# Bidirectional RWKV-7 scan on one core: operands kept at their rows, products as 64x64 quarters and column halves, and a written order for TensorE

## The chip, the cores and the metric

The kernel runs on 1 core of one Trainium2 chip. The metric is device time in microseconds (us), the median of several runs. Before the change it is 1737.47 us, the median of 3 runs that lie between 1731.84 and 1740.01.

## The reference

One layer of a hybrid denoising network works on 128 context tokens and 2048 latent tokens of width 1024. Both sets are RMS-normalised, modulated by a conditioning vector and sent through one input projection. Half of the channels (8 heads of 64) go through RWKV-7 time mixing in both directions in time, the other half through a gated short convolution. The output projection, the residual and a last RMS norm follow. What the change is about is the recurrence over time:

```
def step(S, inp):
    r_t, w_t, k_t, v_t, kk_t, a_t = inp
    s_kk = jnp.einsum('bdhij,bdhj->bdhi', S, kk_t)
    S = (S * w_t[..., None, :] - s_kk[..., :, None] * (kk_t * a_t)[..., None, :]
         + v_t[..., :, None] * k_t[..., None, :])
    return S, jnp.einsum('bdhij,bdhj->bdhi', S, r_t)
...
s_final, ys = lax.scan(step, s0.astype(f32), xs)
...
y = ys[:, 0] + jnp.flip(ys[:, 1], axis=1)
```

A state S is 64x64 for each head and direction. The sum of both directions is normalised by head, weighted, gated and handed to the output projection. The results are y for both token sets and the final context states.

## The kernel before

**Three phases.** Phase 1 does the norms, the input projection, the gates and the low-rank products, and writes what the scan needs to DRAM: `ops{d}` (four operands of each direction d, channel by token, scaled by running products of the decay), `pc{d}` (the decay over a chunk), `vt` (the values, token by channel), `sg`, `q` and the convolution's half of `mixT`. Phase 2 is the scan. Phase 3 multiplies `mixT` by the output weights (psu, lines L1300 to L1302), adds the residual and norms. Each weight there is split into a high and a low part, so a product is three matmuls.

**Stages of the scan.** The scan takes chunks of 64 tokens. A stage is 8 chunks of one pair of heads in both directions (`gi` 0 and 1 are the directions), and there are 17: 16 for the latent tokens, and one, at place 15, for the context of all heads. A stage has six pieces of work:

- partL (L866 on) loads the stage's operands into `rr`, 128 partitions for the two heads of 64 channels.
- partM: ACT copies two operands into block-diagonal 128x128 tiles `bd` (make_bd, a copy for each head), so that one matmul can do both heads. TensorE makes F (psF) and G (psG) of each chunk, both at L905, which DVE masks into `F` and `GA`; it transposes one operand into `Q` (psQ, L898). GA's last 64 columns hold A, the in-chunk interaction of the delta rule. ACT and DVE pick A's diagonal 32x32 blocks (`dg`, L910), and a DMA writes them to DRAM.
- partI: POOL reads all 32x32 blocks of the stage (`ab`) and inverts them as triangular matrices (`zt`, L927 to L948, most of it at L944 and L947). A DMA on POOL's queue writes the inverses to DRAM. partM and partI run LA = 3 stages ahead of the scan.
- partW and partU: the stacked operands `stl` and `str` get their rows from DRAM and, by ACT copies, from GA and Q. `zc` fetches the inverses. psU (L1005) and psW (L1012), 32x32 products in two row tiles, join two 32-blocks into the inverse of a 64-block, which ACT copies into the block-diagonal `zb`.
- partB: psX (L1031) is the inverse times F, copied negated into stl or str by ACT (L790, and L792 for plain copies). psE (L1042) is stl times str, 128x128 for a chunk and head, and DVE masks it into `E` (L1043).
- partS: the scan. psS (L1067) is E times `sv`, whose rows hold the chunk's values and the incoming state. Its one half is the state out, which DVE scales by `pc` into the next chunk's sv (L1080); the other is the chunk's output, added into `y`. When a block of tokens has both directions, finish() does the group norm and transposes y (psT, L1145).

Each psum bank holds four chunks or two chunks of two heads; the pools p2 (psU, psW, psX, psE, psT) have 2 banks, pS (psS) 4, pm (psF, psG, psQ) 2.

**What sets the order.** main() (from L1172) takes a stage's 8 scan steps and between them lets the generators of the other pieces go on: of this stage the rest of partB, of the next stage partW, partU and the first of partB, of stage s+3 partM, and a pending finish. ORDER, ORDER_END and MORD say how many pieces after which step. The order in which each engine then runs its instructions is set by the scheduler of the Tile framework, which simulates a timeline. In the last three stages phase 3 begins: weights() loads the four convolution weights (CONV), ahead() does the convolution half of the products of the first AHEAD = 3 output tiles (psa), and tail() does the rest of the 17 tiles.

Of the kernel before, what the change touches and what calls it, by code (L numbers as in the profile page):

```python
# [6 lines left out]
F32 = mybir.dt.float32  # L7
# [41 lines left out]
def phase1(K):  # L49
# [285 lines left out]

    npair = [0]
# [13 lines left out]
    def mixA(g, j, ws, hh, lw, pre):  # L350

        t0, n = BLK[j]
        nch = n // 64
        tl = lambda tag, b=1: (tp if tag == "sg" else ta_).tile([128, 384], F32, tag=tag, name=f"{tag}_{g}_{j}_{K.u()}", bufs=b)
# [16 lines left out]
        for d in range(2):  # L371
# [32 lines left out]
            nc.scalar.dma_start(S[f"pc{d}"][g * 128:(g + 1) * 128, t0 // 64:t0 // 64 + nch], pt[:, :nch, 64 - 64 * d])  # L404
# [10 lines left out]
            kds.append(kd)  # L415
        bs = kds[0]
# [7 lines left out]
    def gateA(g, j, ws, hh, bsum):  # L424

        t0, n = BLK[j]
        tl = lambda tag, b=1: (tp if tag == "sg" else ta_).tile([128, 384], F32, tag=tag, name=f"{tag}_{g}_{j}_{K.u()}", bufs=b)
# [16 lines left out]
        nc.sync.dma_start(S["vt"][t0:t0 + n, g * 128:(g + 1) * 128].rearrange("(a p) c -> p a c", p=128), vt[:, :n // 128])  # L444
# [242 lines left out]
for _d in range(2):  # L687
    SCR[f"ops{_d}"] = (4, 512, NT)
    SCR[f"pc{_d}"] = (512, 34)
SCR.update(vt=(NT, 512), sg=(512, NT), q=(512, NT), mixT=(1024, NT))  # L690
# [4 lines left out]
MORD = ("Ff", "GgD", "", "Q")  # L695
ON_DVE = ""
# [3 lines left out]
ORDER_END = ('LbbbL', 'UU', 'U', '', 'BBB', '', '', '', '')  # L700
ORDER = ('LbbbL', '', 'U', 'U', 'U', '', 'BBB', '', '')


def phase2(K):
# [3 lines left out]
    MF, MG, ME = (0, 1), (0, 1), (2, 3)  # L708
    B = Ctx()
    O = Ctx()  # L710
    O.scaled = None

    def setup_first():

        O.r0 = Pool(K, "p2r0", "right")
        O.rI = Pool(K, "p2rI", "right")
        O.r1 = Pool(K, "p2r1", "right")
        O.pm = Pool(K, "p2m", "right", 2, PSUM)
        B.msk = O.r0.tile([128, 4, 128], F32, name="msk")
        B.mkg = O.r0.tile([128, 2, 128], F32, name="mkg")  # L720
        for i, j in enumerate((0, 2, 4, 5)):
            D(B.msk[:, i], A["msk"][:, j, 0:128])
        for i, j in enumerate((1, 3)):
            D(B.mkg[:, i], A["msk"][:, j, 64:192])
# [6 lines left out]
        B.slots = []  # L731
        for i in range(2):
            new_slot(O.r0)
        B.bd = ring(O.r1, 2, [128, 8, 128], "bd", zero)
        B.rr = ring(O.r1, 2, [128, 5, 8, 64], "rr", presetR)

    def new_slot(pool):
        i = len(B.slots)
        B.slots.append([tuple(pool.tile([128, 8, w], F32, tag=f"{n}{i}{d}", name=f"{n}{i}{d}", bufs=1) for n, w in (("F", 128), ("GA", 128), ("Q", 64))) for d in range(2)])

    def spare(i, name, dt):

        tags = ["F10", "GA10", "F11", "GA11", "F00", "F01", "GA00", "GA01"]
        if i >= 8:
            return O.rI.tile([128, 1024], dt, tag="ab", name=name, bufs=2)
        return O.r0.tile([128, 1024], dt, tag=tags[i], name=name, bufs=1)

    def setup_rest():
        O.l0 = Pool(K, "p2l0", "left")
        O.l1 = Pool(K, "p2l1", "left")  # L750
        O.p2 = Pool(K, "p2s", "left", 2, PSUM)
        O.pS = Pool(K, "p2S", "left", 4, PSUM)
        O.r2 = Pool(K, "p2r2", "right")
        new_slot(O.r2)
# [8 lines left out]
        for d in range(2):  # L763
            D(B.pc[:, d], S[f"pc{d}"].rearrange("(e c) n -> c e n", c=64))

        lt = ring(O.l1, 2, [128, 2, 8, 128], "stl", lambda t_: presetS(vl(t_)))
        rt = ring(O.l1, 2, [128, 2, 2, 8, 64], "str", presetS)
        B.lt, B.rt = lambda: vl(lt()), rt
        B.bu = O.l1.tile([128, 16, 32], F32, name="bu")
        B.zb = O.l1.tile([128, 2, 8, 128], F32, name="zb")  # L770
        zero(B.zb)

    def ring(pool, n, shape, name, init=None):
        l = [pool.tile(shape, F32, name=f"{name}{i}") for i in range(n)]
        if init:
            for t_ in l:
                init(t_)
        st = [0]

        def get():  # L780
            st[0] += 1
            return l[(st[0] - 1) % n]
        return get

    def copy(k, dst, src, negate=False):
        if negate:
            if k in ON_DVE:
                V.tensor_scalar(dst, src, -1.0, None, ALU.mult)
            else:
                P.activation(dst, src, AF.Copy, scale=-1.0)  # L790
        else:
            (V.tensor_copy if k in ON_DVE else P.copy)(dst, src)  # L792

    def zero(t_):
        G.memset(t_[:], 0.0)

    i2b = lambda n: B.I2[:].unsqueeze(1).broadcast_to((128, n, 64))

    def presetR(t_):
        V.tensor_copy(t_[:, 2], i2b(8))  # L800

    def vl(t_):
        return t_[:].rearrange("p h u (b t) -> p b h u t", b=2)

    def presetS(t_):
        for hd in range(2):
            V.tensor_copy(t_[0:64, 0, hd], B.I2[0:64].unsqueeze(1).broadcast_to((64, 8, 64)))
# [11 lines left out]
    def load(dst, d, k, units, part):  # L819

        a, b = part.start, part.stop
        p, c0 = units[0]
        n = len(units)
        src = S[f"ops{d}"][k]
        if p == units[-1][0]:
            D(dst[part], src[p * 128 + a:p * 128 + b, c0 * 64:(c0 + n) * 64].rearrange("p (u t) -> p u t", t=64))
        else:
            src = src[p * 128:(p + n // 2) * 128, 0:128].rearrange("(g p) t -> p g t", p=128)[part]
            for u in range(2):
                D(dst[part].rearrange("p (g u) t -> p u g t", u=2)[:, u], src[:, :, u * 64:u * 64 + 64])  # L830

    def load_v(dst, units):
        if units[0][0] == units[-1][0]:
            p, c0 = units[0]
            D(dst.rearrange("t u h v -> t u (h v)"), S["vt"][c0 * 64:(c0 + 8) * 64, p * 128:(p + 1) * 128].rearrange("(u t) c -> t u c", t=64))
        else:
            for u in range(2):
                D(dst.rearrange("t (g u) h v -> t u g (h v)", u=2)[:, u], S["vt"][u * 64:u * 64 + 64, :].rearrange("t (g c) -> t g c", g=4))

    H0, H1, FULL = slice(0, 64), slice(64, 128), slice(0, 128)  # L840

    def make_bd(t_, src):
        copy("b", t_[0:64, :, 64:128], src[0:64])
        copy("c", t_[64:128, :, 0:64], src[64:128])

    def load_stk(t_, g, k, us):

        units = g.units[us]
        p, c0 = units[0]
        src = S[f"ops{g.d}"][k]  # L850
        n = 4 if p == units[-1][0] else 2
        for i in range(4 // n):
            dst = t_[0:64, 1, :, us.start + n * i:us.start + n * (i + 1)]
            x = src[(p + i) * 128:(p + i + 1) * 128, c0 * 64:(c0 + n) * 64]
            if t_ is g.rt:
# [571 lines left out]
```

## Time and profile before

| | |
|---|---|
| median of 3 runs | 1737.47 us |
| profiled execution, its own time | 1726.64 us |
| its span | 1724.9 us |
| mean granted TensorE clock | 0.970 |
| TensorE matmul (PE) busy | 1640.9 us, 95% |
| VectorE (DVE), ScalarE (ACT), GpSimd (POOL) busy | 64%, 50%, 34% |
| first scan matmul to last | 1017.3 to 1561 us |

The profile is of one execution. PEld is TensorE's weight load, which runs beside PE. Groups are named by line, engine, operation and `out<-in`, with the busy time and the mean duration of one instruction, and then the engine's idle time ahead of them with what ended it. Matmuls are pipelined, so a duration is longer than the distance from one start to the next. The granted clock is the share of full speed that TensorE was allowed. Rows of the timeline have a start, a length and, in brackets, the idle time before them and its releaser.

### The profile page before, as it was taken

Reading aid. Unit: us, or ns where it says so; the run is one execution under the profiler, and the core shown is the slowest. Engines: PE = TensorE matmul, PEld = TensorE weight load, DVE = VectorE, ACT = ScalarE, POOL = GpSimd, SP = SyncE. Lnnn points to the kernel's source line nnn. Section 1 sums busy time; section 2 is a strip of 40 time slices with the busy share of each in tenths; the row PEclk is TensorE's granted clock in tenths of the full one; section 3 lists DMA queues with packets and bytes.
Section 4 is the critical chain, followed back from the end, with each engine's and each line's share of the span. In section 5 each row is a group of like instructions: output and inputs, shape, how many; then the busy total and the mean of one; then the engine's idle time right before and its main releaser. Section 6 shows DMA issues by size and latency. Waiting matters only on the chain. (4 is left out here: it accounts for less than half of the span.)

```text
span 1724.9 us, 32848 instructions
## 1 busy us (share of the span) xinstructions
PE 1640.9 (95%) x12400; PEld 1556.2 (90%) x12400; DVE 1107.3 (64%) x2092; ACT 868.8 (50%) x1719; POOL 587.4 (34%) x1089
## 2 busy tenths in 40 slices
PE   5989899999999999999999989999999999999998
PEld 2889889899999999999999989999999999887886
DVE  5875778775568858587854344666766656646433
ACT  4533454443243534244423187788878777643222
POOL 0010111111110201021213737877877768223221
PEclk8899999999999999999999999899999989899999
DMA  9687778675557657567896376677878874746442
GB/s 372 212 221 235 223 245 252 199 234 183 173 182 209 176 173 188 167 188 248 208 304 218 112 191 154 163 185 186 203 186 189 189 177 106 195 153 202 147 147 92
DMA packets 314286, 335.66 MB, mean 195 GB/s; under 512 B 165448, under 2 KB 262344, under 8 KB 300048
## 3 DMA queue, kind: packets, MB, share of 16 engines
q1 hardware_dynamic: 277184, 328.97, 65.3%
q10 hardware_dynamic: 35584, 0.14, 1.3%
q0 software_dynamic: 1360, 4.46, 0.7%
q8 instruction: 98, 1.61, 0.4%
q14 instruction: 60, 0.49, 0.1%
HBM read 221.42 MB, written 112.08 MB: 193 GB/s over the span
## 5 line engine op out<-in xcount | busy, mean ns | idle before, releaser
L947 POOL TENSOR_TENSOR zt<-zt,ztmp 128x30 f32<-128x30 f32 (+7 forms) x510 | 198.6, 389 | 39.3
L1067 PE MATMUL psS<-sv,E 128*128 128x64 f32 x1088 | 154.4, 277 | 0.0
L1067 PEld LDWEIGHTS psS<-sv,E 128*128 128x128 f32 x1088 | 145.4, 200 | 1.9
L1042 PE MATMUL psE<-str,stl 128*128 128x128 f32 x1088 | 140.8, 278 | 5.4 <-DVE E L1043 3.8
L944 POOL TENSOR_TENSOR ztmp<-ab,zt 128x60 f32<-128x60 f32 (+7 forms) x255 | 133.5, 524 | 19.4
L1042 PEld LDWEIGHTS psE<-str,stl 128*128 128x128 f32 x1088 | 129.8, 192 | 7.1 <-DVE E L1043 4.8
L323 POOL TENSOR_TENSOR shk<-rawl 128x384 f32<-128x384 f32 (+1 forms) x24 | 23.0, 959 | 322.6 <-ACT rawl L319 322.6
L1080 DVE TENSOR_TENSOR sv<-psS,pc 64x128 f32<-64x128 f32 x254 | 69.4, 277 | 97.3 <-PE psS L1067 96.9
L792 ACT COPY bd<-rr 64x512 f32<-64x512 f32 x136 | 84.0, 617 | 77.2 <-issue 24.5
L1043 DVE TENSOR_TENSOR E<-psE,msk 128x512 f32<-128x512 f32 x136 | 92.9, 685 | 27.6 <-PE psE L1042 26.9
L905 PE MATMUL psF<-rr,bd 128*128 128x128 f32 x544 | 78.8, 291 | 13.0 <-ACT Q L792 10.6
L1363 POOL TENSOR_TENSOR z<-z,x 128x512 f32<-128x512 f32 x32 | 43.6, 1364 | 126.5 <-DVE z L1359 105.8
L905 PEld LDWEIGHTS psF<-rr,bd 128*128 128x128 f32 x544 | 69.2, 199 | 16.3 <-ACT Q L792 13.1
L1031 PE MATMUL psX<-F,zb 128*128 128x128 f32 x544 | 80.7, 303 | 2.7 <-ACT zb L790 1.7
L323 POOL TENSOR_TENSOR shv<-rawl 128x384 f32<-128x384 f32 (+1 forms) x24 | 22.3, 930 | 178.2 <-ACT rawl L319 172.9
L905 PE MATMUL psG<-rr,bd 128*128 128x128 f32 x544 | 74.8, 286 | 2.9 <-DVE F L906 2.9
L1031 PEld LDWEIGHTS psX<-F,zb 128*128 128x128 f32 x544 | 73.7, 214 | 3.6 <-ACT zb L790 2.4
L160 PE MATMUL mmc<-h,w 128*128 128x384 f32 (+1 forms) x192 | 66.7, 347 | 6.8 <-ACT ta L397 3.4
L905 PEld LDWEIGHTS psG<-rr,bd 128*128 128x128 f32 x544 | 68.2, 199 | 3.3 <-DVE F L906 3.0
L161 PE MATMUL mmc<-h,w 128*128 128x384 f32 (+1 forms) x192 | 65.5, 341 | 0.0
L162 PE MATMUL mmc<-h,w 128*128 128x384 f32 (+1 forms) x192 | 65.4, 340 | 0.0
L160 PE MATMUL mmgb<-h,w 128*128 128x384 f32 (+1 forms) x192 | 64.4, 335 | 0.4 <-ACT q1r L321 0.4
(307 smaller groups left out, 5177.2 us busy)
## 6 DMA issues: line engine op xcount, KB each, us to landing
w<-scr_wsp SPq DMA_DIRECT2D x68, 1024.0 KB, 6.7
scr_wsp<-w SPq DMA_DIRECT2D x34, 1024.0 KB, 9.0
rr<-scr_ops SPq DMA_DIRECT2D x64, 512.0 KB, 4.4
scr_ops<-pair SPq DMA_DIRECT2D x80, 384.0 KB, 6.7
wr<-in_win SPq DMA_DIRECT2D x34, 512.0 KB, 6.1
ab<-scr_at SPq DMA_DIRECT2D x34, 256.0 KB, 3.8
x<-in_x SPq DMA_DIRECT2D x17, 512.0 KB, 3.7
wadas<-in_wada SPq DMA_DIRECT2D x8, 1024.0 KB, 14.1
```

Source lines behind the costliest of these rows:

```text
L160: T.matmul(ps[:, :n], w[:, 0, k], hh[:, 0, k, :n], start=k == 0, stop=False)
L161: T.matmul(ps[:, :n], w[:, 0, k], hh[:, 1, k, :n], start=False, stop=False)
L162: T.matmul(ps[:, :n], w[:, 1, k], hh[:, 0, k, :n], start=False, stop=k == 7)
L792: (V.tensor_copy if k in ON_DVE else P.copy)(dst, src)
L905: T.matmul(ps[:, i, :].rearrange("p (a b) -> p a b", b=64), w[:, u, :], x[:, :, u, :], start=True, stop=True)
L944: G.tensor_tensor(tv, ab[:, j:j + 2, j + 2:32].unsqueeze(1).broadcast_to((128, kn, 2, n)), zt[:, :kn, j:j + 2].unsqueeze(3).broadcast_to(( ...
L947: G.tensor_tensor(zt[:, :kn, j + 2:32], zt[:, :kn, j + 2:32], tv[:, :, r], ALU.subtract)
L1031: T.matmul(px[:, i, :], B.zb[:, gi, us.start + i, :], g.F[:, us.start + i, :], start=True, stop=True)
L1042: T.matmul(pe[:, i, hd, :].rearrange("p (b t) -> p b t", b=2), g.lt[:, :, hd, us.start + k + i].rearrange("p b t -> p (b t)"), g.rt[:, :, ...
L1043: V.tensor_tensor(g.E[n][:, k:k + 2].rearrange("p a b c -> p (a b) c"), pe[:].rearrange("p a b c -> p (a b) c"), B.msk[:, ME[g.d]].unsquee ...
L1067: T.matmul(sp[gi][:, q, hd, :], g.E[n][:, k, hd, :], sv[:, u, hd, :], start=True, stop=True)
L1080: r = V.tensor_tensor(dst, sp[gi][0:64, q], B.pc[0:64, d, 2 * p:2 * p + 2, c:c + 1].broadcast_to((64, 2, 64)), ALU.mult)
```

## The change

**Operands at their rows.** rr, bd, stl, str, F and GA slots and Q go. `B.ops` is a ring of four pairs of tiles that hold two operands of a stage, and `B.fg` holds for each direction, for the two sides of E, an identity block and two alternating slots of operands that load_half reads from DRAM a half stage at a time.

**64x64 quarters.** F, G, X and A are made for one head at a time, each head's matmul with 64 rows of weights and 64 columns of the array; place() gives the heads of one direction the straight quarters and those of the other the crossed ones. In the order of issue, both directions and both heads stand side by side, four quarters in turn. The G product's first block is the identity, and so brings what the Q transposes brought. A is a product of its own (psA), made in partM, the only piece left there; F and G move from three stages ahead into the stage before.

**Halves.** E and S are made as two 64-column halves of the array, each with half of the weight columns. ACT copies E's left half, which needs no mask, and DVE masks the right half.

**The order of TensorE.** mm() and tr() tie each matmul of the scan to the one issued before it, by a dependency without a semaphore, so that the scheduler keeps them in the written order. ROUND gives that order for a stage: S is one scan step of both directions, L in turn F and G of the first and second half of the next stage, b and B partB of this and of the next stage (X, or one group of E), u the transpose of the inverses and psU psW in turn with U, A partM, f three pieces of finish and T the rest of it.

**Buffers and queues.** p2 gets 3 banks and pS 3; zt 3 buffers (2 before), the A blocks' dg 2 (1). The chunk decays pc go by a POOL copy into a tile and one SP DMA for each pair of token blocks; before, 48 DMAs on ACT's queue. vt is stored by head pair, two DMAs of 64 partitions for one.

**Phase 3.** The convolution weights are loaded and split one at a time in ahead(), AHEAD falls to 2 tiles, and what frees them buffers changes.

```diff
-MORD = ("Ff", "GgD", "", "Q")
-ORDER_END = ('LbbbL', 'UU', 'U', '', 'BBB', '', '', '', '')
-ORDER = ('LbbbL', '', 'U', 'U', 'U', '', 'BBB', '', '')
+ROUND = "f A b L L S u b S b S L S U S L U S T S B S B B".split()
+ROUND_END = "f b L L u S b S b S L U S L S U S T S B B B S".split()
...
-    O.p2 = Pool(K, "p2s", "left", 2, PSUM)
-    O.pS = Pool(K, "p2S", "left", 4, PSUM)
+    O.p2 = Pool(K, "p2s", "left", 3, PSUM)
+    O.pS = Pool(K, "p2S", "left", 3, PSUM)
...
+    def behind(r, ins):
+        if ins is not None:
+            tc.add_manual_dep(r.ins, ins.name, mybir.DependencyInfo(mybir.DependencyClass.NoSync, mybir.DependencyReason.DATA), reason="order")
+    def mm(*a, **k):
+        r = T.matmul(*a, start=True, stop=True, **k)
+        if O.line:
+            behind(r, O.last)
+            O.last = r.ins
...
+    def place(d, h):
+        return H[1 - h if d == 0 else h]
...
     def partM(s, st):
+        pa = [O.pm.tile([128, 8, 64], F32, tag="m", name=f"psA{s}_{gi}") for gi in range(2)]
+        for u in range(8):
+            for gi, g in enumerate(st.g):
+                for h in range(2):
+                    mm(pa[gi][place(g.d, h), u, :], g.ops[H[h], 1, u, :], g.ops[H[h], 0, u, :])
+        yield
...
+            P.activation(dg[:], pa[gi][:, :, 0:32], AF.Identity, scale=B.hm[:, 0:1])
+            V.scalar_tensor_tensor(dg[:], pa[gi][:, :, 32:64], B.hm[:, 1:2], dg[:], ALU.mult, ALU.add)
+            copy(st.low[:, gi], pa[gi][:, :, 32:64])
+            D(at[gi * 8:gi * 8 + 8].rearrange("u s b j i -> (s b j) u i"), dg[:])
...
     def partW(s, st):
+            def product(k, x, nm):
+                ps = [O.p2.tile([128, 4, 128], F32, tag="s", name=f"ps{nm}{s}_{gi}_{n}") for gi in range(2)]
+                for i in range(4):
+                    for gi, g in enumerate(st.g):
+                        u = half(g, n).start + i
+                        for h in range(2):
+                            mm(ps[gi][place(g.d, h), i, :].rearrange("p (b t) -> p b t", b=2), g.ops[H[h], k, u, :], B.fg[g.d][H[h], x, g.io, h, u])
+                return ps
+            ps = product(0, 1, "F")
...
+            ps = product(1, 0, "G")
+            for gi, g in enumerate(st.g):
+                us = half(g, n)
+                for h in range(2):
+                    r = place(g.d, h)
+                    copy(g.gs[H[1 - h], 0, h, us], ps[gi][r, :, 0:64])
+                    V.tensor_tensor(g.gs[H[1 - h], g.op, h, us], ps[gi][r, :, 64:128], B.msk[r, MG[g.d], 64:128].unsqueeze(1).broadcast_to((64, 4, 64)), ALU.mult)
...
     def partB(s, st):
...
+                        for hd in range(2):
+                            for x in range(2):
+                                mm(pe[H[x], i, hd, :].rearrange("p (b t) -> p b t", b=2), lt[:, x * g.op, hd, u], rt[:, g.io, hd, u])
...
+                    copy(to(H[0]), of(H[0]))
+                    V.tensor_tensor(to(H[1]), of(H[1]), B.msk[:, ME[g.d], 64:128].unsqueeze(1).broadcast_to((128, 4, 64)), ALU.mult)
...
     def partS(s, st, nxt):
...
-                    T.matmul(sp[gi][:, q, hd, :], g.E[n][:, k, hd, :], sv[:, u, hd, :], start=True, stop=True)
+                    for x in H:
+                        mm(sp[gi][x, q, hd, :], g.E[n][:, k, hd, x], sv[:, u, hd, :])
...
-    AHEAD = TILES[:3]
+    AHEAD = TILES[:2]
```

On PE, in the scan of stage 7, the order before is the scheduler's. The names are psum tile, stage, direction (0 or 1) and half; the tiles after the arrow are the operands, and the last figures their shape and a count.

```order
L1067 MATMUL psS7_0_0_12996<-sv_1027_12520,E_1041_12802 128x64 x2
L1031 MATMUL psX7_1_1_12951<-F11_8820,zb_9831 128x128 x4
L1067 MATMUL psS7_1_0_13000<-sv_1028_12529,E_1042_12810 128x64 x2
L905 MATMUL psF10_1_0_13067<-rr1_8828,bd0_8823 128x128 x4
L905 MATMUL psF10_1_1_13073<-rr1_8828,bd0_8823 128x128 x3
L1067 MATMUL psS7_0_0_12996<-sv_1027_12520,E_1041_12802 128x64 x2
L905 MATMUL psF10_1_1_13073<-rr1_8828,bd0_8823 128x128
L1042 MATMUL psE7_0_10_12958<-str0_9824,stl0_9818 128x128 x4
```

After the change, at the same place of the same stage, PE's order reads:

```order
L780 MATMUL psG8_0_0_13947<-fg0_9774,o00_8854 64x128 x2
L780 MATMUL psG8_1_0_13948<-fg1_9775,o01_8855 64x128 x2
L780 MATMUL psS7_0_0_13973<-sv_1063_13382,E_1073_13710 64x64 x4
L780 MATMUL psS7_1_0_13979<-sv_1064_13384,E_1074_13713 64x64 x4
L780 MATMUL psE7_0_10_13987<-fg0_9774 64x128 x8
L780 MATMUL psE7_1_10_13998<-fg1_9775 64x128 x8
L780 MATMUL psS7_0_0_13973<-sv_1063_13382,E_1073_13710 64x64 x4
L780 MATMUL psS7_1_0_13979<-sv_1064_13384,E_1074_13713 64x64 x4
```

F and G of stage 10 stood between the scan steps of stage 7; now it is those of stage 8, pairs of quarters of the two directions follow each other, and groups of E stand whole between whole scan steps.

ACT has, before, this stretch of copies around the same scan steps (L790 negates, L792 copies; w and yss belong to finish):

```order
L790 ACTIVATE stl0_9818<-psX7_0_0_12803 64x2x4x64 x2
L790 ACTIVATE str1_9825<-psX7_1_0_12811 64x2x256 x2
L1128 ACTIVATE w_1054_13038<-y_1018_12326 128x512
L1132 ACTIVATE yss_1056_13054<-yss_1056_13054,geps_9813 128x8
L792 COPY bd1_8824<-rr1_8828 64x8x64 x2
L792 COPY str0_9824<-Q20_9805 64x2x2x64
L792 COPY str0_9824<-GA20_9804 64x256 x2
L792 COPY str0_9824<-Q20_9805 64x2x2x64
```

After, ACT's order at the start of stage 7's round is this (a0 takes A's lower blocks, which psU needs; fg takes both X and G):

```order
L771 COPY E_1074_13713<-psE7_1_01_13761 128x4x64
L839 ACTIVATE dg_1083_13878<-psA10_0_13844,hm_8852 128x256
L839 ACTIVATE dg_1084_13883<-psA10_1_13845,hm_8852 128x256
L771 COPY a0_8862<-psA10_0_13844 128x256
L771 COPY a0_8862<-psA10_1_13845 128x256
L769 ACTIVATE fg0_9774<-psX7_0_1_13888 64x2x256 x2
L769 ACTIVATE fg1_9775<-psX7_1_1_13889 64x2x256 x2
L972 ACTIVATE zb_9784<-zc_1089_13922,hm_8852 128x16x32 x2
L771 COPY fg0_9774<-psG8_0_0_13947 64x256
```

The copies into bd and from Q are gone, the two reads of A, four of X and the halves of E are the group that stands there now; all but zb read a psum bank.

More of the change, by code (lines that the diff above doesn't have):

```diff
@@ L805, in presetS @@
-    def presetS(t_):
-        for hd in range(2):
-            V.tensor_copy(t_[0:64, 0, hd], B.I2[0:64].unsqueeze(1).broadcast_to((64, 8, 64)))
+            P.activation(dst, src, AF.Copy, scale=-1.0)
+        else:
+            P.copy(dst, src)
+    def behind(r, ins):
[6 more added lines that the diff above has]
+            O.last = r.ins
@@ L809, in tl, with tr @@
+    def tr(*a):
+        r = T.transpose(*a)
+        if O.line:
+            behind(r, O.last)
+            O.last = r.ins
     def tl(shape, tag, b, pool=None, dt=F32):
@@ L817, in phase2 @@
     stages.insert(15, [(d, [(u // 2, u % 2) for u in range(8)], None) for d in range(2)])
[L819 to L855, printed above, removed]
-                D(dst.rearrange("c h u t -> c h (u t)"), x.rearrange("(h c) t -> c h t", h=2))
-            else:
-                for hd in range(2):
-                    D(dst[:, hd], x[hd * 64:hd * 64 + 64].rearrange("c (u t) -> c u t", t=64))
+    def place(d, h):
+        return H[1 - h if d == 0 else h]
     def half(g, n):
@@ L1004, in partU @@
             for r0, r1 in rows:
-                T.matmul(pu[r1, u, :], st.g[u // 8].GA[r0, u % 8, 96:128], st.zr[r0, u, :], start=True, stop=True)
+                mm(pu[r1, u, :], st.low[r0, u // 8, u % 8], zr[r0, u, :])
         for r0, r1 in rows:
-            copy("u", B.bu[r1], pu[r1])
+            copy(zr[r1], pu[r1])
         yield
```

284 lines of the change are left out of this document (126 added, 158 removed).

## The prediction

> **What bounds the kernel now.** I read the page first, then PE busy time by stage, then the groups and the order in time of one round of the scan.
>
> ```profile
> span 1724.9 us, 32848 instructions
> PE 1640.9 (95%) x12400; PEld 1556.2 (90%) x12400; DVE 1107.3 (64%) x2092; ACT 868.8 (50%) x1719; POOL 587.4 (34%) x1089
> 885.00:985.50 100.50, 98.48 (x699) 98.24 (x698) 40.09 (x80) 21.62 (x40) 47.65 (x102) 0.98 0.61 204
> 985.50:1017.30 31.80, 24.62 (x275) 22.85 (x274) 14.11 (x28) 22.35 (x45) 5.17 (x11) 0.84 0.82 197
> 1017.30:1456.10 438.80, 425.12 (x5054) 414.53 (x5053) 273.83 (x563) 348.24 (x666) 336.07 (x754) 0.96 0.73 175
> 1456.10:1528.40 72.30, 67.77 (x662) 62.04 (x662) 41.02 (x82) 47.00 (x87) 25.50 (x48) 0.91 0.59 161
> 1528.40:1724.90 196.50, 187.23 (x878) 154.01 (x877) 95.20 (x166) 52.84 (x126) 48.27 (x34) 0.99 0.44 150
> L1067 PE MATMUL psS<-sv,E 128*128 128x64 f32 x896 | 126.6, 276 | 0.0
> ```
>
> After start, length and colon the stretches list busy time of PE, PEld, DVE, ACT, POOL, then granted clock. 896 psS records are 14 rounds of 64, so the fifth stretch is 14 rounds of 31.34 us, with PE busy 97%, ACT 79%, POOL 77%. TensorE is the bound from 885 to the end. A program matmul in f32 is two records.
>
> ```profile
> 1213.35 1.95 PE L1042 MATMUL psE<-str,stl 128*128 128x128 f32 x16
> 1215.13 0.56 PE L1067 MATMUL psS<-sv,E 128*128 128x64 f32 x4
> 1215.53 2.00 PE L905 MATMUL psG<-rr,bd 128*128 128x128 f32 x16
> 1219.15 1.00 PE L1067 MATMUL psS<-sv,E 128*128 128x64 f32 x8
> 1219.99 0.61 PE L898 MATMUL psQ<-idt,rr 128*128 128x128 f32 x4
> 1221.43 1.20 PE L1005 MATMUL psU<-zr,GA 32*32 32x32 f32 x64
> 1222.56 1.10 PE L1067 MATMUL psS<-sv,E 128*128 128x64 f32 x8
> ```
>
> From start to next start, a 128x128 record costs 0.111 us (1.78 by 16), an S record 0.105 though it streams half the columns, so its 128-column weight load sets it, and a 32x32 record 0.018.
>
> **The change part by part.** *Quarters and halves.* The trace has no 64x64 tile; the nearest rows are column tiles of 32.
>
> ```profile
> 34.47 1.06 PE L190 MATMUL psrow<-wadas,scp 128*32 128x512 f32 x8
> 35.46 0.44 PE L161 MATMUL mmf<-h,w 128*128 128x384 f32 x1
> 84.80 1.05 PE L190 MATMUL psgr<-wgate,scp 128*32 128x512 f32 x4
> 85.78 0.45 PE L160 MATMUL mmk<-h,w 128*128 128x384 f32 x1
> ```
>
> Four column tiles (8 records) take 0.99 us, two (4 records) 0.98: column tiles run beside each other. psU, two 32-row tiles at a time, takes 0.018 a record where a quarter of 0.111 is 0.028: two row tiles overlap as well, in different columns. Row tiles in the same columns no row shows. Bounds: four quarters at once 0.028 us a record, two at once 0.056. I take 0.028, as both directions overlap by themselves.
>
> A round before: F, G, X 96 records and E 64 by 0.111, S 64 by 0.105, Q 8, U and W 128 by 0.018: 28.0 us. After: A 64 records of half length 0.9; F, G, X 192 by 0.028, 5.4; E 128 halves, two at once, 7.1; S 128 halves of half length and half load, 3.6; U, W 2.3; output transposes 0.5: 19.8. Two at once, it is 26.1.
>
> *Tile changes.* The fixed round goes about 14 times between quarters, halves and small tiles.
>
> ```profile
> 1224.57 0.24 PE L1012 MATMUL psW<-zc,bu 32*32 32x32 f32 x2
> 1224.74 0.66 PE L1067 MATMUL psS<-sv,E 128*128 128x64 f32 x4
> 1225.33 1.19 PE L1012 MATMUL psW<-zc,bu 32*32 32x32 f32 x62
> ```
>
> Here four S records between two W pieces took 0.59, against 0.40 between psE and psG at 1215.13: two changes, 0.2 us, so 14 cost 1.4 to 2.1. The Trainium skill, TensorEngine Tiling (Array Packing), section Tiling Modes, says that a change of tiling mode drains the engine; the trace agrees, at 0.1 us.
>
> *The round in its fixed order.* With 21.5 us of work (19.8 and about 1.7) TensorE no longer bounds a round; the chain over the evacuations does: each group waits until ACT or DVE has read an earlier one, and since PE takes its groups in the fixed order, whatever stands behind a waiting group waits too. Their rows:
>
> ```profile
> L1043 DVE TENSOR_TENSOR E<-psE,msk 128x512 f32<-128x512 f32 x112 | 76.5, 684 | 15.6 <-PE psE L1042 15.2
> L1080 DVE TENSOR_TENSOR sv<-psS,pc 64x128 f32<-64x128 f32 x218 | 59.6, 277 | 89.1 <-PE psS L1067 88.7
> L790 ACT ACTIVATE stl<-psX 64x512 f32<-64x512 f32 x56 | 33.1, 591 | 22.2 <-PE psX L1031 21.5
> L792 ACT COPY str<-Q 64x256 f32<-64x256 f32 x57 | 23.0, 403 | 3.8 <-PE psE L1042 2.8
> L910 ACT ACTIVATE dg<-GA,hm 128x256 f32<-128x256 f32 x28 | 14.2, 509 | 1.0 <-DVE GA L906 0.3
> L792 ACT COPY bd<-rr 64x512 f32<-64x512 f32 x104 | 64.2, 617 | 35.9 <-issue 13.9 <-DMA rr<-scr_ops 7.9 <-PE psG L905 3.7
> 1013.62 1.16 PE L1042 MATMUL psE<-str,stl 128*128 128x128 f32 x8 [0.90 <-ACT stl L790]
> 1014.82 0.69 DVE L1043 TENSOR_TENSOR E<-psE,msk 128x512 f32<-128x512 f32 x1 [1.37 <-PE psE L1042]
> ```
>
> A 256-wide mask is 0.41 (between 277 and 684 by width), a 256-wide copy 0.40. From a product's last issue (1013.62 plus 8 by 0.111) to its reader is 0.3 us. I walk one round with three buffers for F, G, X, E, U, W, T. E of the first half: 0 to 3.9, A to 4.95, X to 5.85. ACT then has two dg, two low copies (1.8) and four X copies (2.4): the first X bank is free at 8.4, so F, next on PE, waits 2.7 us. F to 9.4; G waits for the second X bank and F's mask, to 11.4; S0 to 12.0; E, S1, E, S2, each behind a mask or scale, to 17.05; F to 18.1, S3 to 18.9, U to 20.15; S4 waits for scales behind two F masks and two y adds, to 21.55; G, W to 23.85; S5, T, S6 to 26.05; X to 27.1, S7 to 28.3; the next E waits for X's copies, 28.9. So 28.9 at full clock, though ACT loses the eight bd (617 ns), eight stl and eight str copies (403 ns) a round. For rows before and after the clock:
>
> ```profile
> 1034.12:1037.53 3.41, 3.05 (x81) 2.83 (x80) 0.65 (x3) 2.65 (x6) 2.94 (x7) 1.00 1.13 250
> 1037.53:1040.95 3.42, 3.42 (x18) 3.42 (x18) 0.77 (x3) 1.51 (x3) 1.63 (x4) 0.50 0.60 167
> 1095.56:1098.97 3.41, 2.51 (x76) 2.21 (x74) 2.03 (x5) 3.27 (x9) 2.94 (x7) 1.00 0.90 181
> 1098.97:1109.21 10.24, 10.24 (x100) 9.77 (x101) 1.73 (x5) 4.03 (x7) 6.46 (x17) 0.50 0.41 126
> 1205.40:1235.50 30.10, 29.40 (x367) 28.84 (x366) 20.92 (x44) 24.45 (x48) 25.41 (x58) 1.00 0.82 201
> ```
>
> A stretch of 3.4 us with PE busy 89% or 74%, but mostly 32x32 tiles (76 to 81 records), is followed by half clock for 3.4 or 10.2 us. Rounds at full clock take 30.1, so the clock costs 1.2 of 31.34. After, the F wait, and U and W with S, are such stretches. I take 1.1 us: 30.0 a round, 14 rounds gain 19 us.
>
> The skill's TensorE: Matmul & The Clock Gate, HAM oscillation, asks only for no idle gap over about 3.4 us. By that the clock would stay full, the round 28.9 and the time 16 us lower; the rows above disagree, since their stretches were never idle so long.
>
> *Before the scan.* F, G and Q of stages 0 and 1 leave the preparation, where PE is full; A takes their place.
>
> ```profile
> L905 PE MATMUL psF<-rr,bd 128*128 128x128 f32 x69 | 10.0, 299 | 2.0 <-DMA rr<-scr_ops 2.0
> L905 PE MATMUL psG<-rr,bd 128*128 128x128 f32 x64 | 8.1, 275 | 0.0
> L898 PE MATMUL psQ<-idt,rr 128*128 128x128 f32 x16 | 2.4, 272 | 0.0
> ```
>
> 144 records by 0.111 (five of psF belong to stage 2) less A's 2.2 (two stages by 0.9, and four tile changes): minus 14 us. From there to the first S, 31.8 before, I keep: loads, U, W, X, E still follow each other. The pc stores leave ACT's queue for small POOL copies and a twelfth of the DMAs, the vt stores double on SP: nothing, as PE is full there; if PE waited for SP, 24 issues would cost some us.
>
> *The end.* Rounds 14 and 15 and the 48 output products moved into 13 and 14 (11 us, mostly in waits): 63 against 72.3, minus 9; before, round 15 waited for the last inversion, which now ends earlier.
>
> ```profile
> 1548.09 0.39 PE L1302 MATMUL psu<-woh,mla 128*128 128x512 f32 x1
> 1548.32 0.39 PE L1300 MATMUL psu<-woh,mha 128*128 128x512 f32 x1
> ```
>
> An output record costs 0.23 from start to start. From S16 on, with two tiles ahead in place of three, 24 more of them (two halves, four rows of weights, three products each), 5.5; 4 us for the last group norm's transposes, which now stand ahead of the first output product; 1 for the clock: plus 10.5.
>
> Sum: minus 14, 19 and 9, plus 10.5: minus 31.5, so span 1693.4. The profiled execution took 1726.64, 10.8 under the median of 1737.47; carried over, 1706.
>
> **The rivals.** *The round falls to POOL's pace*, if the waits overlap better than I walked. POOL's busy time is 24.0 a round (336.07 by 14), with gaps about 28: minus 28 us, 1678. For it: the preparation's end lets POOL start early. Against: ACT's queue behind A and X.
>
> *Quarters run two at a time.* F, G, X, A take 6.3 us more of PE, about 5 on the chain: round 35, 16 rounds, plus 80, 1786, slower. It decides above a round of 33. psU's overlap in one bank speaks against it. Array Packing, Restrictions and Gotchas, says that different row tiles can't access one PSUM bank at once, and both quarters of a unit write one bank; by that rule this rival holds.
>
> *Half clock takes hold.* Two such stretches a round, each slowing 3 us of chain work to half, make the round 33: plus 48, 1754, slower. For it: PE's work falls from 90% to 70% of the round. Against: E, full work, is spread over it.
>
> *The round is merely reordered*: 32 us, PE's gain turned into evacuation waits, plus 30, about 1737.
>
> **How the numbers follow.** Forecast (rounds 28.9 to 31.2, 1688 to 1724) 0.54; POOL's pace 0.17; no gain 0.11; two at a time 0.07; half clock 0.11. Within 0.5%, about what can be told from no change, is 1728.8 to 1746.2. Faster 0.71, same 0.11, slower 0.18. The range 1668 to 1752 leaves out two at a time and the outer half of the clock case, and a little below.
>
> **What would show it.** Right: quarter records at about 0.028 from start to start, PE busy near 75% of a round, F waiting for X copies by ACT, round near 30, the last output product some 10 us later after S16 began. Wrong: quarters at 0.056, or granted clock under 0.9 over the rounds, or zc arriving last in each round.

## The result and the profile after

The changed kernel took 1693.32 us, the median of 4 runs from 1690.45 to 1698.55; the kernel before took 1734.65 beside it. The ratio is 0.9762, with a 95% interval of 0.9724 to 0.98. The forecast was 1706 and faster. The profiled execution has a span of 1696.7 us, 28.2 less than before, where the forecast's sum said 31.5 less. The medians lie 41 us apart: the profiled execution of before was 8 us faster than its median and that of after 5 us slower, so the stretches below account for 28 us and not for all 41. The total was about right, but two of its terms were badly wrong, with opposite signs.

The page's first rows after the change, and its psE and psF groups, answer to the rows that the prediction quoted:

```profile
span 1696.7 us, 42079 instructions
PE 1551.0 (91%) x17160; PEld 1419.1 (84%) x17160; DVE 1076.9 (63%) x2156; ACT 743.7 (44%) x1547; POOL 619.8 (37%) x1134
L780 PE MATMUL psE<-fg 128*64 128x128 f32 x2176 | 153.3, 294 | 32.3 <-ACT fg L769 20.7
L780 PE MATMUL psF<-fg,o 64*64 64x128 f32 x1088 | 50.8, 289 | 32.9 <-ACT fg L769 26.9
```

PE is busy 90 us less, and its products now wait for ACT most of all. Where the 28 us come from is read in stretches. Of before, rounds 0 to 11, and 12 and 13, apart (the columns are those of the prediction's stretches):

```profile
1017.30:1395.10 377.80, 366.39 (x4358) 357.43 (x4357) 237.09 (x486) 300.01 (x573) 292.60 (x655) 0.96 0.74 180
1395.10:1456.10 61.00, 58.73 (x698) 57.09 (x697) 36.73 (x79) 48.23 (x94) 43.48 (x100) 0.94 0.63 146
```

Of after, the end of the preparation, from there to the first S, rounds 0 to 11, 12 and 13, 14 and 15, and from S16 to the end:

```profile
885.00:950.50 65.50, 65.50 (x510) 65.18 (x509) 23.64 (x52) 5.45 (x13) 43.94 (x90) 1.00 0.58 176
950.50:989.50 39.00, 27.29 (x579) 23.83 (x577) 16.48 (x35) 17.34 (x37) 22.40 (x51) 0.80 0.81 188
989.50:1349.30 359.80, 304.32 (x7718) 264.05 (x7716) 213.96 (x534) 212.20 (x454) 275.42 (x622) 0.93 0.61 154
1349.30:1428.90 79.60, 64.95 (x1276) 52.79 (x1274) 39.56 (x92) 43.17 (x87) 64.30 (x131) 0.85 0.50 130
1428.90:1488.30 59.40, 46.12 (x1076) 39.76 (x1074) 35.03 (x87) 30.37 (x63) 7.12 (x13) 0.89 0.29 85
1488.30:1696.70 208.40, 194.73 (x1002) 157.28 (x1000) 97.59 (x171) 55.07 (x132) 47.90 (x34) 0.96 0.42 145
```

| stretch | before | after | difference | forecast |
|---|---|---|---|---|
| start to first S | 1017.3 | 989.5 | -27.8 | -14 |
| rounds 0 to 11 | 377.8 | 359.8 | -18.0 | -16 (12 of 14 rounds) |
| rounds 12 and 13 | 61.0 | 79.6 | +18.6 | -3 (2 of 14) |
| rounds 14 and 15 | 72.3 | 59.4 | -12.9 | -9 |
| S16 to the end | 196.5 | 208.4 | +11.9 | +10.5 |

Twelve rounds of 29.98 us stand against the forecast 30.0. PE is busy in 304.32 of their 359.8 us, 85%, where the forecast had named 75% as a sign of being right. A typical one, on PE:

```profile
1184.41 1.10 PE L780 MATMUL psX<-F,zb 64*64 64x128 f32 x32
1185.44 0.69 PE L780 MATMUL psS<-sv,E 128*64 128x64 f32 x16
...
1192.10 1.16 PE L780 MATMUL psA<-o 64*64 64x64 f32 x64
1193.08 1.06 PE L780 MATMUL psX<-F,zb 64*64 64x128 f32 x32
1193.96 0.39 PE L780 MATMUL psF<-fg,o 64*64 64x128 f32 x4
1196.35 1.09 PE L780 MATMUL psF<-fg,o 64*64 64x128 f32 x28 [2.00 <-ACT fg L769]
```

32 quarter records take 1.03 us to the next start (1184.41 to 1185.44), 0.032 a record with a tile change in it; without one, from X to F (1193.08 to 1193.96), 32 take 0.88, 0.0275 a record. That is a quarter of the 0.111 of a full record: four at once. F waits 2.00 us for X's copies, where the walk had 2.7.

### The profile page after: what moved, and what is told of

Same layout as the page of the kernel before. It is cut to its first block, busy times and chain, and to the rows that moved or that the text cites. A ratio compares the mean times of both kernels' runs of the same rounds, so it can differ in the third digit from the quotient of the medians.

```text
span 1696.7 us, 42079 instructions
## 1 busy us (share of the span) xinstructions
PE 1551.0 (91%) x17160; PEld 1419.1 (84%) x17160; DVE 1076.9 (63%) x2156; ACT 743.7 (44%) x1547; POOL 619.8 (37%) x1134
## 4 chain that ended last, share of the span: by engine, by line
PE 61%; DVE 17%; ACT 8%; DMA 7%; issue 3%; POOL 2%; SPq 1%; DVEq 0%; ACTq 0%; POOLq 0%
PE psE L780 6%; PE psu L1267 4%; PE psu L1268 4%; PE psu L1269 4%; ACT fg L769 4%; PE psS L780 3%; PE psG L780 2%; PE mmv L160 2%; PE mmv L161 2%; PE mmv L162 2%; DVE fg L949 2%; PE mmg L161 1%; PE mmg L162 1%; PE mmg L160 1%; PE mmc L160 1%
## 5 line engine op out<-in xcount | busy, mean ns | idle before, releaser
L780 PE MATMUL psE<-fg 128*64 128x128 f32 x2176 | 153.3, 294 | 32.3 <-ACT fg L769 20.7
L780 PEld LDWEIGHTS psE<-fg 128*64 128x64 f32 x2176 | 130.9, 149 | 46.9 <-ACT fg L769 33.2
L780 PE MATMUL psS<-sv,E 128*64 128x64 f32 x2176 | 104.1, 238 | 13.3 <-DVE sv L1046 8.8
L780 PEld LDWEIGHTS psS<-sv,E 128*64 128x64 f32 x2176 | 85.0, 146 | 32.8 <-DVE sv L1046 14.4
L1009 DVE TENSOR_TENSOR E<-psE,msk 128x256 f32<-128x256 f32 x136 | 55.8, 419 | 60.7 <-ACT E L771 59.8
L769 ACT ACTIVATE fg<-psX 64x512 f32<-64x512 f32 x136 | 80.6, 592 | 20.6 <-PE psX L780 18.2
L949 DVE TENSOR_TENSOR fg<-psG,msk 64x256 f32<-64x256 f32 x136 | 57.2, 421 | 43.3 <-ACT fg L771 40.8
L780 PE MATMUL psF<-fg,o 64*64 64x128 f32 x1088 | 50.8, 289 | 32.9 <-ACT fg L769 26.9
L160 PE MATMUL mmc<-h,w 128*128 128x384 f32 (+1 forms) x192 | 65.4, 341 | 5.8 <-ACT q1r L321 2.9
L771 ACT COPY fg<-psG 64x256 f32<-64x256 f32 x136 | 50.0, 367 | 38.1 <-PE psG L780 28.8
L162 PE MATMUL mmc<-h,w 128*128 128x384 f32 (+1 forms) x192 | 64.0, 333 | 0.0
```

The costliest lines, as they stand in the source:

```text
L160: T.matmul(ps[:, :n], w[:, 0, k], hh[:, 0, k, :n], start=k == 0, stop=False)
L162: T.matmul(ps[:, :n], w[:, 1, k], hh[:, 0, k, :n], start=False, stop=k == 7)
L771: P.copy(dst, src)
L780: r = T.matmul(*a, start=True, stop=True, **k)
L949: V.tensor_tensor(g.gs[H[1 - h], g.op, h, us], ps[gi][r, :, 64:128], B.msk[r, MG[g.d], 64:128].unsqueeze(1).broadcast_to((64, 4, 64)), ALU ...
```

## The experiments

**Where the preparation's 28 us are from.** The first two runs move the pc stores alone. In the changed kernel they are put back:

```diff
-            G.tensor_copy(pcs[:, d, c0 - pc0:c0 - pc0 + nch], pt[:, :nch, 64 - 64 * d])
+            nc.scalar.dma_start(S[f"pc{d}"][g * 128:(g + 1) * 128, t0 // 64:t0 // 64 + nch], pt[:, :nch, 64 - 64 * d])
...
-        if j % 2:
-            nc.sync.dma_start(S["pc"][g * 128:(g + 1) * 128, :, pc0:c0 + nch], pcs[:, :, :c0 + nch - pc0])
```

> The changed kernel, with the chunk decays pc stored as before (48 DMAs on ACT's queue, elements of 4 bytes). Theory (the first 335 us were short because these small packets no longer load the DMA engines while the input weights are fetched): the 16 us come back between 80 and 480 us, the first scan matmul goes from 989.5 back to about 1005, and the time rises by 14 to 16 us to about 1708. Rival (the preparation is shorter by what the scan's set-up no longer does, or by the values' new layout): no change beyond 3 us, first scan matmul at 988 to 992.

It took 1718.28 us, 0.9934 of before (0.991 to 0.9958). The same diff the other way round, in the kernel before:

> The kernel before, with only the pc stores changed: POOL copies and 12 SP DMAs for the 48 on ACT's queue. Theory (DMA load of small packets): first scan matmul 14 to 16 us earlier, near 1002, and the time near 1719. Rival (set-up or values' layout): within 3 us of before.

It took 1703.61 us, 0.9843 of before (0.981 to 0.9877). So this one edit is worth 1.6% in the old kernel, and in the new one what lies between 0.9762 and 0.9934, 1.7%: 27 to 30 us, nearly twice what was expected of it, and over half of the whole gain. Everything else in the change is worth 0.7% (0.9934) to 0.8% (0.9762 against 0.9843). The first scan matmul comes at 1011.3 us with the old stores in the new kernel and at 989.5 without them; in the old kernel at 1017.3 with them and at 992.4 without. The stretch from 80 to 340 us shows where 14 of these 22 to 25 us come from, first of before:

```profile
80.00:340.00 260.00, 244.66 (x1342) 230.03 (x1341) 195.16 (x340) 119.51 (x224) 36.34 (x35) 0.99 0.79 232
q1 hardware_dynamic: 21846, 60.14, 76.1%
q10 hardware_dynamic: 10976, 0.04, 3.0%
ACT w L125 <- DMA wr<-in_win: 30.6, 10, 10.1
DVE pair L401 <- DMA scr_ops<-pair: 26.1, 8, 4.9
```

And of before with the new pc stores:

```profile
80.00:340.00 260.00, 258.60 (x1450) 246.05 (x1449) 217.75 (x376) 133.13 (x248) 56.97 (x52) 1.00 0.70 248
q1 hardware_dynamic: 23930, 64.29, 69.5%
ACT w L125 <- DMA wr<-in_win: 11.7, 6, 4.2
```

Queue rows list packets, MB and the share of 16 engines' time; wait rows list total, count and longest. The 10976 small packets carry 0.04 MB and take 3.0% themselves; but the large transfers on q1 take 1.27% of the time per MB beside them (76.1 by 60.14) and 1.08% without (69.5 by 64.29). ACT waits 30.6 us for input weights with them, 11.7 without. DVE waits 26.1 us until its operands' spills (pair) have landed with them, and not at all here without. PE, which the prediction called full, gains 14 us of work in this stretch (244.66 to 258.60).

Two more runs ask what of it counts. One leaves 48 issues on ACT's queue and makes the elements long, with the copies on ACT and their tile in place of pp as the source; the other leaves the short elements and takes the issues off ACT's queue and the source off pp:

```diff
-            G.tensor_copy(pcs[:, d, c0 - pc0:c0 - pc0 + nch], pt[:, :nch, 64 - 64 * d])
+            P.copy(pcs[:, d, c0 - pc0:c0 - pc0 + nch], pt[:, :nch, 64 - 64 * d])
+            nc.scalar.dma_start(S["pc"][g * 128:(g + 1) * 128, d, c0:c0 + nch], pcs[:, d, c0 - pc0:c0 - pc0 + nch])
```

> The changed kernel, with the chunk decays copied by ACT and stored in 48 DMAs on ACT's queue as before, but from a dense tile, so each element is 24 bytes or more. Theory (the number of packets is what cost 28 us): within 4 us of the changed kernel. Rival (the 48 issues on ACT's queue and what stands behind them): 15 us or more slower, as with the old stores, and more by 48 copies.

```diff
-            pcsum[g] = tp.tile([128, 2, 12], F32, tag="pcs", name=f"pcs{g}_{j}", bufs=2)
+            pcsum[g] = tp.tile([128, 12, 2], F32, tag="pcs", name=f"pcs{g}_{j}", bufs=2)
...
-            nc.sync.dma_start(S["pc"][g * 128:(g + 1) * 128, :, pc0:c0 + nch], pcs[:, :, :c0 + nch - pc0])
+            for d in range(2):
+                nc.sync.dma_start(S["pc"][g * 128:(g + 1) * 128, d, pc0:c0 + nch], pcs[:, :c0 + nch - pc0, d])
```

> The changed kernel, with the POOL copies as they are and 24 SP DMAs from a tile in which the two directions alternate, so each element has 4 bytes again: as many packets as before the change, but neither on ACT's queue nor on the pp tiles. Theory (packets): 20 to 28 us slower than the changed kernel, first scan matmul near 1010. Rival (ACT's queue, or pp held by the DMA): within 4 us of the changed kernel.

Their base is the changed kernel, run again beside them:

> The changed kernel as it is, as the base for the runs beside it. All theories: about 0.976 of the kernel before.

The base has 0.9737 of before (0.9703 to 0.9771), long elements from ACT's queue 0.9737 (0.9707 to 0.9767), short elements from SP 1.0322 (1.0294 to 1.035). Taken with this second base, the old stores cost up to 2.0% and everything else is worth up to 1.1%. So 48 issues on ACT's queue cost nothing, and short elements are enough to cost time. One part of the old stores is not separated: they also held pp. In the old kernel ACT stood 10 us in four waits until such a store had landed, and the run with long elements took that away too. On SP's queue as many short elements cost 100 us, far more than the 20 to 28 expected, and PE has only 231.81 us of work in the stretch:

```profile
80.00:340.00 260.00, 231.81 (x1261) 218.19 (x1259) 183.21 (x314) 111.93 (x209) 43.28 (x44) 0.93 0.82 226
q1 hardware_dynamic: 30528, 58.43, 81.2%
DVE pair L406 <- DMA scr_ops<-pair: 35.3, 3, 13.7
```

The weights, spills and short elements share one queue there, and DVE waits up to 13.7 us at a time for a spill, where no such wait was over 4.9 in the kernel before. That the spills stand behind the short elements in the queue is argued, not shown.

**Rounds 12 and 13.** On PE, ACT and SP of the changed kernel, where round 12 stands still:

```profile
1381.37 5.56 PE L780 MATMUL psE<-fg 128*64 128x128 f32 x48 [9.08 <-ACT fg L769]
1379.65 1.05 ACT L1247 CAST woh<-woraw 128x1024 fp32r<-128x1024 f32 x1 [8.96 <-DMA woraw<-in_wout]
1380.72 1.21 ACT L769 ACTIVATE fg<-psX 64x512 f32<-64x512 f32 x2
1371.69 0.37 SPq L1241 DMA_DIRECT2D woraw<-in_wout  x1
```

The cast of an output weight stands ahead of two of X's copies in ACT's order, its load was issued only at 1371.69, and ACT does the copies only after it. PE waits 9.08 us for them. The next run fetches the same weights earlier, and splits two of them then:

```diff
+    def prep():
+        O.r = Pool(K, "p3r", "right")
+        O.raw = {k: load_raw(k) for k in CONV[2:]}
+        yield
+        for k in CONV[2:]:
+            load_k(k, *[O.r.tile([128, 1024], F32R, name=f"wo{a}{k}") for a in "hl"], V, O.raw[k])
+            O.raw[k - 2] = load_raw(k - 2)
+            yield
...
+            if s == 6:
+                prep = K.prep()
+            if s in (6, 8, 10):
+                next(prep)
```

> The changed kernel, with the four convolution weights of the output projection fetched in stages 6 to 10 instead of 14 on, and two of them split then, so that no cast on ACT waits for its load in round 12. Theory (ACT stood 8.96 us in front of the X copies because the cast of a weight waited for its DMA): the waits of 9.08 and most of the other excess of rounds 12 and 13 (44.5 and 35.0 us against 30) go, rounds 12 and 13 together about 67 us, the time 9 to 13 us lower, near 1682. Rival (the output products themselves fill these rounds, 48 by 0.23 us, and the last inversion sets the end): the rounds fall by less than 4 us, the time stays within 3 us.

It took 1680.25 us, 0.971 of before (0.968 to 0.974). Its stretch of rounds 12 and 13:

```profile
1340.60:1409.90 69.30, 62.34 (x1276) 51.78 (x1274) 38.21 (x90) 41.32 (x85) 59.66 (x122) 0.91 0.55 135
```

69.3 us for 79.6, against about 67 expected: the wait is gone, and what is left over two rounds of 30 is 9.3 us, near the 11 us of the 48 output products; that it is theirs is inferred from the size. This kernel has the lowest ratio so far. Its interval meets those of the changed kernel (0.9762 and 0.9737), so the 10 us rest on the stretch as much as on the ratio.

**The chain of a round.** Two orders try to fill F's wait. X ahead of A:

```diff
-ROUND = "f A b L L S u b S b S L S U S L U S T S B S B B".split()
+ROUND = "f b A L L S u b S b S L S U S L U S T S B S B B".split()
```

> The changed kernel, with X ahead of A in each round of the written order. Theory (the wait of 2.00 us that F has in every round is for X's copies, which stand on ACT behind four reads of A): F waits under 0.8 us, the round falls from 30.0 by 1.2 to 2 us, 13 rounds gain 15 to 25 us, time near 1673. Rival (POOL's inversion, begun 2.4 us later in each round, or the clock takes it back): the round stays within 0.5 us of 30, with zc arriving last or the granted clock lower.

It took 1703.33 us, 0.9847 (0.9825 to 0.9869): slower than the changed kernel, and the rounds from 986.9 to 1359.3 take 372.4, 31.0 each. F's wait went, and another came behind it; PE and DVE in this kernel:

```profile
1199.48 1.54 PE L780 MATMUL psG<-fg,o 64*64 64x128 f32 x28 [2.66 <-DVE F L941]
1197.95 0.88 DVE L840 SCALAR_TENSOR_TENSOR dg<-psA,hm,dg 128x256 f32<-128x256 f32 x2 [4.23 <-ACT dg L839]
1198.75 1.28 DVE L941 TENSOR_TENSOR F<-psF,msk 128x512 f32<-128x512 f32 x2
```

DVE stood 4.23 us in front of A's dg with F's masks behind it, since ACT came to its part of dg only after X's copies. F's wait fell as the theory said, but neither it nor the rivals had this wait. The second order puts S and A into the two waits:

```diff
-ROUND = "f A b L L S u b S b S L S U S L U S T S B S B B".split()
+ROUND = "f b S L A L u b S b S L S U S L U S T S B S B B".split()
```

> The changed kernel, with each round in the order f b S L A L in place of f A b L L S: X, the first scan step, F, A, G. Theory (the wait of F for X's copies is filled by S, that of G for F's masks by A, and DVE meets F's masks before A's dg): the round falls by 1 to 2 us to 28.5, 13 rounds gain 13 to 25 us. Rival (a later reader is late instead: G's copies on ACT behind dg and the low copies, or POOL, whose inversion starts 4 us later in the round): the round stays at 30 or grows, as with X ahead of A.

0.9744 (0.9718 to 0.9771): no change, 29.9 us a round. The waits of PE in its rounds and in those of the base, where the columns are total, count and longest:

```profile
PE psE L780 <- DVE fg L949: 18.0, 10, 2.0
PE psF L780 <- ACT fg L769: 2.7, 11, 0.3
```

```profile
PE psF L780 <- ACT fg L769: 22.0, 11, 2.0
PE psE L780 <- DVE fg L949: 1.3, 3, 0.4
```

The 2 us moved from F to the E behind G. In both orders the wait came back further down, so what sets this part is, as these waits read, the chain itself (X, its copies, F, its masks, G, its copy and mask, E).

**Quarters two at a time.** The heads become the outermost loop of F, G, X and A, here F and G:

```diff
-                for i in range(4):
-                    for gi, g in enumerate(st.g):
-                        u = half(g, n).start + i
-                        for h in range(2):
+                for h in range(2):
+                    for i in range(4):
+                        for gi, g in enumerate(st.g):
+                            u = half(g, n).start + i
```

> The changed kernel, with the quarters of F, G, X and A issued head by head: only the two directions of one head are neighbours, so two different quarters alternate where four did. Theory (quarters overlap only with their neighbours in the order of issue; four at once is worth what the forecast set against two): 0.056 us a record for 0.031, PE in a round about 5 us more, the round 33 to 35 and the time 50 to 80 us higher, near 1760. Rival (the round's length is that of the chain over ACT and DVE, and the slower products go into its waits): the time within 15 us.

It took 1764.17 us, 1.0212 of before (1.0167 to 1.0256), and 32 records now take 1.52 us for 1.03, in an otherwise equal place:

```profile
1209.29 1.59 PE L780 MATMUL psF<-fg,o 64*64 64x128 f32 x32
1210.81 0.69 PE L780 MATMUL psS<-sv,E 128*64 128x64 f32 x16
```

The rounds are 34.4 us (413.3 by 12). The order in which quarters are issued is worth 70 to 80 us here: with two neighbours in place of four the whole change would be a loss, though a smaller one than the rival's 1786. A record takes 0.0475 with a tile change in it, less than the 0.056 of strictly two at once; why is not shown.

**Without the written order.**

```diff
-        O.line = True
```

> The changed kernel without the ties between matmuls, so that the scheduler orders TensorE in the scan as it did before the change. Theory (the evacuations set the round, and the written order costs the 2.0 us that F waits): the scheduler puts other work there, the round falls by about 1 us and the time by 10 to 15 us. Rival (the written order keeps quarters and halves together, and the scheduler breaks them up into more tile changes and runs of one quarter): the round rises by 1 to 3 us, the time by 15 to 50 us.

1698.5 us, 0.9844 (0.9796 to 0.9893). Rounds 0 to 11 lost nothing by it, 354.2 us or 29.5 each:

```profile
984.60:1338.80 354.20, 333.19 (x7716) 286.31 (x7711) 219.16 (x536) 209.84 (x454) 274.83 (x616) 1.00 0.60 155
```

The difference in the total is small: its interval just meets the changed kernel's first one (0.9724 to 0.98) and lies above the second (0.9703 to 0.9771), its profiled span of 1693.5 lies between their 1696.7 and 1690.2, and rounds 14 and 15 take 74 us (from 1411.4 to 1485.4) for 59.4. In the steady rounds the gain is 0.5 us, half of what the theory said, and comes with a clock of 1.00; 21 of the 48 output products stand in rounds 14 and 15 there and none in the changed kernel, and rounds 12 and 13 take 72.6 us for 79.6, so a part of the loss at the end is work moved there; the rest is open.

**The clock.** In the kernel with the weights early, matmuls of the identity are put in front of the first F and the first E of a round, as extra work that the products overwrite (the fillers):

```diff
+                for _ in range(7 if nm == "F" and n == 0 else 0):
+                    mm(ps[0][:, 0, :], B.idt[:], B.idt[:])
...
+                    for _ in range(6 if n == 0 and h2 == 0 and gi == 0 else 0):
+                        mm(pe[:, 0, 0, :], B.idt[:], B.idt[:])
```

> The changed kernel with the weights early, and in each round 7 matmuls of the identity by itself in front of the first F and 6 in front of the first E, 128x128, into banks that the products then overwrite; they are extra work. Theory (the half clock of a round follows the windows in which F and the first E wait, and such windows cost 1.2 us a round): half clock falls from 31 us in eleven rounds to under 10, the round from 29.8 to about 28.8, the time by 10 to 16 us to about 1666 (0.963 of before). Rival (the chain over ACT and DVE alone sets the round; or the fillers push the products back): within 4 us of the kernel without them, 0.971 of before, or slower by up to 13 rounds of 1 us.

It took 1684.56 us, 0.9759 (0.9713 to 0.9805): no gain over 0.971. Rounds 0 to 11 without the fillers, and with them:

```profile
984.30:1340.60 356.30, 297.32 (x7718) 255.83 (x7716) 213.59 (x534) 211.95 (x454) 277.74 (x625) 0.95 0.61 156
```

```profile
988.60:1340.90 352.30, 321.85 (x8030) 279.63 (x8028) 213.67 (x534) 211.30 (x453) 272.27 (x615) 1.00 0.60 155
1340.90:1417.10 76.20, 67.96 (x1328) 56.14 (x1326) 39.02 (x90) 42.20 (x87) 65.38 (x137) 0.96 0.54 132
```

With the waits of F and E filled the clock is full, so the half clock did come from these windows; but ending it was worth 0.33 us a round net of what the fillers cost (29.69 to 29.36), not 1.1. That most of the half clock lay beside waits for ACT and DVE, which a faster PE does not shorten, is argued, not shown. In rounds 12 and 13, which have the output products to do, the fillers cost 6.9 us (76.2 for 69.3).

**E's mask in one piece.** The last run has the weights early, and gives E back to DVE as before the change:

```diff
-                    copy(to(H[0]), of(H[0]))
-                    V.tensor_tensor(to(H[1]), of(H[1]), B.msk[:, ME[g.d], 64:128].unsqueeze(1).broadcast_to((128, 4, 64)), ALU.mult)
+                    V.tensor_tensor(g.E[n][:, k:k + 2].rearrange("p a b c -> p (a b) c"), pe[:].rearrange("p a b c -> p (a b) c"),
+                                    B.msk[:, ME[g.d]].unsqueeze(1).broadcast_to((128, 4, 128)), ALU.mult)
```

> The changed kernel with the weights early, and with E masked by DVE alone, 128x512 in one go as before the change, in place of ACT's copy of the left half and DVE's mask of the right. Theory (the two halves do not run beside each other: the masks' idle time before them, 38.3 us of 88 masks, is ended by ACT's copy, so halving bought no latency, 0.37 plus 0.42 against 0.69): waits of E for a mask fall, ACT loses 3 us a round, the round falls by 0.3 to 1 us and the time by 4 to 12 us from 0.971 of before. Rival (DVE has 2 us a round more and its F and G masks are late): the round rises by 0.3 to 1.5 us, the time by 4 to 20 us.

1679.85 us, 0.9702 (0.9673 to 0.9731) against 0.971: no difference that can be told. In the changed kernel the half masks do stand behind the copies:

```profile
L1009 DVE TENSOR_TENSOR E<-psE,msk 128x256 f32<-128x256 f32 x96 | 39.4, 420 | 42.3 <-ACT E L771 41.8
```

41.8 us of idle time ahead of 96 masks end with ACT's copy, so the halves follow each other. Splitting E between two engines neither gains nor costs here.

## Why the prediction was right in the time, and where its steps failed

- **Quarters at 0.028 us, four at once:** right, 0.0275 without a tile change and 0.032 with one. Both quarters of a unit write one bank, so the rule of the Trainium skill (TensorEngine Tiling (Array Packing), Restrictions and Gotchas) under which they would go two at a time does not hold for these 32 records; two neighbours took 1.52 us for 32, and the price of that rival (plus 80 us on the sum) came out as 70 to 80.
- **The walk of a round:** right in its mechanism. F waits 2.00 us for X's copies (2.7 forecast), the round is 29.98 (30.0), and POOL, the pace of one rival, is busy 23 us of it. That 30.0 was met so closely is partly luck: in the two runs at full clock the round is 29.4 and 29.5 and not 28.9, and the clock's share 0.3 to 0.5 and not 1.1. Neither run changes the clock alone. (The round's work before adds up to 27.7 and not 28.0; nothing hangs on it.)
- **The clock:** the rule of the Trainium skill (TensorE: Matmul & The Clock Gate, HAM oscillation) would have had it full, as no gap in a round is near 3.4 us; PE's longest wait in rounds 0 to 11 is 2.5. The granted clock there is 0.93, so the rows that spoke against the rule were the better guide.
- **"Nothing, as PE is full there"**, said of the pc stores: this step failed, by 22 to 25 us in the preparation. The prediction goes by one stretch of it, 885 to 985 us; from 80 to 340 PE was busy 94%, and ACT stood 30.6 us before input weights there. The page's queue rows have 35584 packets for 0.14 MB, 1.3% of the engines' time, for these stores; the prediction did not price them, and that share would have been far too low a price.
- **F, G and Q leave the preparation, minus 14:** right by itself. With the old stores kept, PE is full until 972.7 in place of 985.5, 13 us. But the stretch to the first S, held at 31.8, became 39.0: F and G now stand in it, and PE waits there 5.98 us for their operands, at 957.81, where the same wait cost 2.0 before:

```profile
957.81 2.25 PE L780 MATMUL psF<-fg,o 64*64 64x128 f32 x17 [5.98 <-DMA fg<-scr_ops]
```

- **The output products "mostly in waits":** failed. Rounds 12 and 13 rose by 18.6 us where 3 less was forecast. 10.3 of it went with the early weights, so it was ACT's wait for a weight, which the prediction had not named; the rest is about what the products themselves take.
- **The end:** plus 11.9 for 10.5, and rounds 14 and 15 minus 12.9 for 9.

So 14 us more gain than forecast before the first S and 22 us more loss in rounds 12 and 13 nearly cancelled: that the total came out was luck, and it hid two wrong causes. The stores of 0.14 MB are worth 1.6 to 2.0%. Everything else, which the forecast credited with all of the time, is worth 0.7 to 1.1%: the scan gains 18.0 us in its first twelve rounds, and rounds 12 and 13 lose 18.6.

## What to carry to other kernels

Price a DMA by its packets and by who waits for the transfers beside it, not by its bytes or its own share: 48 stores with 4-byte elements cost at least 1.6% of this kernel. An in-order engine that serves a tight chain should meet no instruction whose load may be late; fetch it rounds ahead. When a chain over several engines sets the pace, filling one wait can move it to the next link, as both orders did here, so time the chain's end and not the wait.

## What the hardware showed beyond that

- Four 64x64 tiles in neighbouring issues run at 0.032 us a record of 128 columns, two at 0.0475, a tile change included in both; only the order of issue differs.
- Half clock on PE can cost little: from 0.95 to 1.00 in twelve rounds gained 4.0 us of 356, the fillers included.
- As many 4-byte elements cost 27 to 30 us on ACT's queue and 100 us on the queue that carries the weights.
